# A hybrid decoder layer on one core: weight tiles as two half tiles, a planner constant for loads behind copies, and other buffers for the output projection's rows

## The chip, the cores and the metric

The kernel runs on one core of one Trainium2 chip. The metric is the device time of one execution in microseconds; the median of three runs counts.

## What is computed

One decoder layer on 1024 tokens of width 1024, in float32. The input is normalised, multiplied by one wide weight matrix, and its columns go to three branches and a gate:

```python
h = _rmsnorm(x, g_in[l])
proj = h @ w_in[l]
q_sb, k_sb, v_sb, u_c, b_c, c_c, q_mem, gate = jnp.split(proj, SPLIT_POINTS, axis=-1)
y_sb = _stick_breaking_attention(...)            # 8 heads of 64, strictly causal
y_conv = b_c * _causal_depthwise_conv(c_c * u_c, conv_w[l], conv_b[l])
m = _rmsnorm(mem, g_mem[l])
mk, mv = jnp.split(m @ w_mem_kv[l], 2, axis=-1)  # 256 memory tokens
y_mem = _memory_attention(...)                   # 4 heads of 64, softmax
y = jnp.concatenate([_rmsnorm(y_sb, g_sb_out[l]), _rmsnorm(y_conv, g_conv_out[l]),
                     _rmsnorm(y_mem, g_mem_out[l])], axis=-1)
x = x + (y * jax.nn.silu(gate)) @ w_out[l]
return _rmsnorm(x, g_final)
```

The weight of a stick-breaking head is A[t,s] = sigmoid(z_ts) times the product of 1 - sigmoid(z_tj) over the keys j between s and t.

## The kernel before

**The order is made by a planner.** The functions of the kernel don't issue instructions: each call is recorded as an `Op` with an engine (or two to choose from, `nc.either`: VectorE or GpSimd), a priority `prio`, and the ops that it needs. `Plan.lay_out` then plays the program through once with modelled durations: whenever an engine is idle it takes, of the ops whose inputs are there and whose tiles have a free buffer (`room`), the one with the lowest `prio`. `emit` issues the instructions in that order, so each engine has a fixed order when the kernel runs, and a wait of one instruction holds back all that stand behind it on its engine. Buffers of one tag are given out in the order of the program (`turn`, `nth`), except for tiles marked `loose`.

**The model of a DMA.** All DMAs are issued by SyncE. One of them takes `ISSUE` on SyncE, then its bytes go over one modelled wire, behind those before it, at the first of `RATES` (405, in KB per us) from or to DRAM and at the second (225) between two places of SBUF; `LANDING` comes on top.

**The work.** Matmuls are made more exact by splitting each operand in a high and a low part (`hi` is a rounded copy made by ScalarE, `lo` the rest, made by VectorE or GpSimd) and adding three products. A projection (`proj`) is one weight tile of 128 columns: `load_w` loads 512 KB into `wraw` (one buffer), splits it by halves into `whi` and `wlo` (two buffers each), and 48 matmuls of 512 columns add into two PSUM banks `pj`. At the start (the loop over `KC`) x comes in eight chunks; the first q and k projections (`w0`) and half of the values grow chunk by chunk.

Attention goes by pairs of heads. For a head, `stacks` copies q and k from natural layout (`qh`, `ql`, `kh`, `kl`) into the tiles `q`, `qs` and `k` by DMAs within SBUF, 256 KB each. `scores` makes score matmuls into PSUM banks `z` (two), sigmoids on ScalarE, a scan on VectorE; `apply` transposes the result through banks `tr` and multiplies with the values into banks `av` (two). Projections stand as fill between them, at a later priority (`FILL`).

`stats` sums the squares of one row block of y with a matmul by ones into a PSUM bank (`z`, loose); ScalarE reads it and four small DMAs spread the sums. `gate` is a projection whose evacuation multiplies with y. The last gate runs over the chunks of x one after another, so that the buffers `X` of x come free as it goes.

The end is the output projection. Each of eight row blocks of `w_out` is loaded into a raw buffer named by `RAW` (tags qh, ql, qh, ql, whi, whi, wlo, wlo), split into `woh` and `wol`, which from the second block on lie in buffers `X`, and 8 token blocks `j` are multiplied with all of them into the banks pj, z and tr.

Of the kernel before, what the change touches and what calls it, by code (L numbers as in the profile page):

```python
# [24 lines left out]
F32 = mybir.dt.float32  # L25
# [132 lines left out]
class Op:  # L158
    __slots__ = ("n", "engines", "call", "args", "kw", "prio", "needs", "then", "left", "tiles", "ready",
                 "table", "start", "engine", "nbytes", "cost", "port", "at")  # L160

# [19 lines left out]

ISSUE, RATES, LANDING, UNDER_WAY = 0.6, (405.0, 225.0), 1.35, 8
PATIENCE = 2.5


class Plan:
# [7 lines left out]
    def record(self, engines, call, args, kw):  # L194
# [41 lines left out]
        if call == "matmul":  # L236
            width = int(np.prod(kw["rhs"].shape[1:]))
            o.cost = {"tensor": width * 0.00042 + 0.014 if width > P else 0.1}
        elif call == "transpose":
            o.cost = {"tensor": 0.089}  # L240
        elif call == "dma_start":
            o.cost = {engines[0]: ISSUE}
            inside = all(isinstance(kw[x], View) and kw[x].tile.pool.name != "dram" for x in ("in_", "out"))
            o.nbytes = o.nbytes / 1024 / RATES[inside]
        elif call == "memset":
            o.cost = {e: 0.1 + 0.0011 * width for e in engines}
        else:
            pointers = sum(isinstance(kw.get(k), View) for k in ("scale", "bias"))
            wide = max([width] + [int(np.prod(v.shape[1:])) for v in ins]) if call == "tensor_reduce" else width
            o.cost = {"vector": 0.16 + 0.00105 * wide, "gpsimd": 0.18 + 0.00218 * wide,  # L250
                      "scalar": 0.18 + 0.00086 * wide + (0.09 if pointers else 0) + (0.2 if "accum_out" in kw else 0)}
            if call == "tensor_tensor_scan":
                o.cost = {"vector": 0.16 + 0.00208 * width}
            elif call == "scalar_tensor_tensor":
                o.cost = {e: c + 0.06 for e, c in o.cost.items()}
            elif kw.get("op") == ALU.pow:
                o.cost["gpsimd"] = 0.8 + 0.12 * width

            o.port = engines[0] in ("vector", "gpsimd") and len(ins) > 1 and not inpsum
# [4 lines left out]
    def lay_out(self):  # L264
# [3 lines left out]
        idle = dict.fromkeys(ready, 0.0)  # L268
        events, table, wire, landed = [], None, 0.0, []
        done, now, port = 0, 0.0, {"vector": 0.0, "gpsimd": 0.0}  # L270
# [38 lines left out]
        while done < len(self.ops):  # L309
            for e in ready:  # L310
                while idle[e] <= now:
# [22 lines left out]
                    if o.call == "dma_start":  # L334
                        wire = max(wire, begin + ISSUE) + o.nbytes
                        end = wire + LANDING
                        landed.append(end)
                    else:
                        end = begin + cost
# [44 lines left out]
def hymba_kernel(ctx, tc, xT, xr, wp, wv, memT, memr, wmem, cols, eye, wout, gfin, out):  # L384
# [3 lines left out]
    xpool = Pool(nc, "xpool", {"X": 16})  # L388
    wring = Pool(nc, "wring", {"wraw": 1, "whi": 2, "wlo": 2})
    stg = Pool(nc, "stg", {"stg": 4})  # L390
# [64 lines left out]
    w0 = []  # L455
    for pool, tag in ((wring, "wraw"), (att, "k")):
        w0.append((pool.tile([P, KC, P], F32, tag, "w0"), wring.tile([P, KC, P], F32R, "whi"),
                   wring.tile([P, KC, P], F32R, "wlo")))
    ps0 = [[bank("z"), bank("z")], [bank("pj"), bank("pj")]]
    for k in range(KC):  # L460
# [11 lines left out]
        for n in range(2):  # L472
            if k in (0, 2, 4):
                c = slice(k, KC if k == 4 else k + 2)
                nc.sync.dma_start(out=w0[n][0][:, c], in_=wp[4 * n][:, c])
        for n, c in enumerate(parts):
# [7 lines left out]
        if k in (0, 2, 4):  # L484
            for raw, hi, lo in w0:
                c = slice(k, KC if k == 4 else k + 2)
                nc.scalar.copy(hi[:, c], raw[:, c])
# [8 lines left out]
        def column(n, i):  # L496
            for a, (ww, xx) in enumerate(((w0[n][1], h), (w0[n][1], l), (w0[n][2], h))):
                nc.tensor.matmul(ps0[n][i], lhsT=ww[:, k, :], rhs=xx[:, HALVES[i]], start=(k == 0 and a == 0),
                                 stop=(k == KC - 1 and a == 2))
# [39 lines left out]
    fills = [0]  # L539

    def load_w(src, shape, prio=None, raw=None):
        prio = prio or SPLIT + fills[0]
        hi = wring.tile(shape, F32R, "whi")
        lo = wring.tile(shape, F32R, "wlo")
        raw = att.tile(shape, F32, raw, "wraw") if raw else wring.tile(shape, F32, "wraw")
        n = shape[1] // 2
        parts = [slice(0, n), slice(n, 2 * n)]
        for c, x in zip(parts if isinstance(src, list) else [slice(0, 2 * n)], src if isinstance(src, list) else [src]):
            nc.sync.dma_start(out=raw[:, c], in_=x, prio=prio)
        for c in parts:  # L550
            nc.scalar.copy(hi[:, c], raw[:, c], prio=prio)
            nc.either.tensor_tensor(lo[:, c], raw[:, c], f(hi[:, c]), op=ALU.subtract, prio=prio)
        return hi, lo

    def more_values():
# [3 lines left out]
        for jj in range(4):  # L559
            ps = bank("pj")  # L560
            for j in (2 * jj, 2 * jj + 1):
                for k in range(KC):
                    wh, wl = w[k // 4]
                    for a, (xx, ww) in enumerate(((xh, wh), (xh, wl), (xl, wh))):
                        nc.tensor.matmul(ps[:, (j % 2) * 256 : (j % 2 + 1) * 256], lhsT=xx[k][:, j * P : (j + 1) * P],
                                         rhs=ww[:, k % 4, :], start=(k == 0 and a == 0), stop=(k == KC - 1 and a == 2),
                                         prio=FILL + fills[0] + 0.1 * jj)
# [5 lines left out]
    def proj(n, evac, after=(), both=False):  # L573
# [7 lines left out]
        for i, k in steps:  # L581
            hf = HALVES[i]
            for a, (ww, xx) in enumerate(((wh, xh), (wh, xl), (wl, xh))):
                first = k == 0 and a == 0
                nc.tensor.matmul(ps[i], lhsT=ww[:, k, :], rhs=xx[k][:, hf], start=first,
                                 stop=(k == KC - 1 and a == 2), prio=FILL + fills[0] + (0 if both else 0.4 * i),
# [146 lines left out]
    def stats(c, late=False):  # L733
# [5 lines left out]
        for n, hf in enumerate(HALVES):  # L739
# [5 lines left out]
            nc.either.tensor_tensor(lo, s, f(hi), op=ALU.subtract)  # L745
            ps = psum.tile([P, H], F32, "z", loose=True)
            for b, w in enumerate((hi, lo)):
# [88 lines left out]
    def mem_kv():  # L836
# [10 lines left out]
        for k2 in range(4):  # L847
# [13 lines left out]
            for m in range(2):  # L861
                for kk in range(2):
                    for a, (ww, mm) in enumerate(((wh, mh), (wl, mh), (wh, ml))):
                        nc.tensor.matmul(acc[m], lhsT=mm[:, kk, m * P : (m + 1) * P], rhs=ww[:, kk, :],
                                         start=(k2 == 0 and kk == 0 and a == 0), stop=(k2 == 3 and kk == 1 and a == 2))
# [83 lines left out]
    woh, wol = [None] * 8, [None] * 8  # L949
    RAW = [(att, t) for t in ("qh", "ql", "qh", "ql")] + [(wring, t) for t in ("whi", "whi", "wlo", "wlo")]  # L950
    for n, c in enumerate(order):
# [3 lines left out]
        lo = pool.tile([P, D], F32R, tag, "wol")  # L955
        raw = RAW[n][0].tile([P, D], F32, RAW[n][1], "wor")
        nc.sync.dma_start(out=raw, in_=wout[c])
        for hf in HALVES:
            nc.scalar.copy(hi[:, hf], raw[:, hf])
            nc.either.tensor_tensor(lo[:, hf], raw[:, hf], f(hi[:, hf]), op=ALU.subtract)  # L960
        woh[c], wol[c] = hi, lo
# [97 lines left out]
```

## Time and profile before

| what | value |
|---|---|
| runs, us | 566.96, 568.11, 568.99 |
| median, us | 568.11 |
| profiled execution, us | 569.42 |
| its span, from the first to the last instruction, us | 567.4 |
| mean granted TensorE clock of the span | 0.996 |
| TensorE matmuls, share of the span | 97% |
| VectorE, ScalarE, GpSimd, share of the span | 73%, 63%, 33% |
| DMA queue of SyncE, share of 16 engines' span | 35.8% |

The profile shows one execution. Matmuls are pipelined: each is shown from its start to a modelled end, and neighbours overlap, so that the distance of two starts tells what a matmul takes. All instructions that the planner issues carry one line number, so groups are told apart by the tiles that they write and read (written <- read).

### The profile page before, as it was taken

What the parts mean: (1) busy time and instruction counts of PE and PEld (TensorE: products, weight loads), DVE (VectorE), ACT (ScalarE), POOL (GpSimd) and SP (SyncE); (2) the same over time, 40 slices, a digit from 0 to 9 for tenths busy, and PEclk for the clock granted to TensorE, in tenths of its full rate; (3) what the DMA queues carried; (4) which work ended last, traced back from release to release, by engine and by line L of the source; (5) the groups of instructions that cost most, each with busy time, mean ns of one, the idle gap of its engine ahead of it and who ended that gap; (6) DMA issues with size and microseconds to landing.
All of it is one profiled execution on the core that took longest, in us unless ns stands there. A gap on an engine that the chain in (4) does not pass through costs nothing.

```text
span 567.4 us, 8661 instructions
## 1 busy us (share of the span) xinstructions
PE 552.4 (97%) x2984; PEld 467.4 (82%) x2984; DVE 415.6 (73%) x658; ACT 355.9 (63%) x726; POOL 186.5 (33%) x214
## 2 busy tenths in 40 slices
PE   8999899999999999999899999999999999999995
PEld 6998789998888888888788878888878686888884
DVE  3345488878888798767497778769787678876673
ACT  5834577787677674785378797765689945332322
POOL 1220133332445534532063363212533239010010
PEclk9999999999999999999999999999999999999998
DMA  8953915043160711017732511443511342223301
GB/s 264 396 162 80 218 38 131 20 92 97 37 149 1 185 39 37 13 42 161 189 99 75 131 38 53 96 109 95 170 39 37 88 141 107 74 75 112 112 37 74
DMA packets 30655, 58.35 MB, mean 103 GB/s; under 512 B 13202, under 2 KB 14226, under 8 KB 30612
## 3 DMA queue, kind: packets, MB, share of 16 engines
q1 hardware_dynamic: 30612, 57.81, 35.8%
q8 instruction: 23, 0.38, 0.3%
q14 instruction: 20, 0.16, 0.1%
HBM read 36.78 MB, written 4.20 MB: 72 GB/s over the span
## 4 chain that ended last, share of the span: by engine, by line
PE 84%; DMA 6%; issue 3%; DVE 2%; ACT 2%; SPq 2%; POOL 1%; POOLq 0%; DVEq 0%; ACTq 0%
PE pj L380 49%; PE tr L380 14%; PE z L380 12%; PE av L380 9%; SPq L380 2%; DMA xs<-in_xT 2%; DMA q<-ql 1%; DMA stg<-in_wv 1%; DMA wraw<-in_wmem 1%; DMA gf<-in_gfin 1%; DVE stg L380 1%; DVE wlo L380 0%; ACT whi L380 0%; POOL wlo L380 0%; DMA part<-sq 0%
## 5 line engine op out<-in xcount | busy, mean ns | idle before, releaser
L380 PE MATMUL pj<-xh,whi 128*128 128x512 f32 x368 | 146.0, 397 | 1.2 <-DVE y L380 1.2
L380 PE MATMUL pj<-xl,whi 128*128 128x512 f32 x368 | 146.3, 398 | 0.0
L380 PE MATMUL pj<-xh,wlo 128*128 128x512 f32 x368 | 145.2, 395 | 0.0
L380 POOL TENSOR_TENSOR sg<-sg,F 128x512 f32<-128x512 f32 (+5 forms) x58 | 63.2, 1095 | 87.8 <-DVE F L380 60.1
L380 PEld LDWEIGHTS pj<-xh,whi 128*128 128x128 f32 x368 | 69.2, 188 | 14.5 <-DVE y L380 1.7
L380 PEld LDWEIGHTS pj<-xh,wlo 128*128 128x128 f32 x368 | 69.3, 188 | 12.3 <-issue 0.2
L380 PEld LDWEIGHTS pj<-xl,whi 128*128 128x128 f32 x368 | 69.3, 188 | 11.9 <-issue 0.2
L380 ACT ACTIVATE sg<-z,rq 128x511 f32<-128x511 f32 (+2 forms) x96 | 56.0, 583 | 36.1 <-PE z L380 31.3
L380 DVE TENSOR_TENSOR_SCAN F<-z,mask 128x512 f32<-128x512 f32 (+2 forms) x64 | 60.5, 949 | 19.4 <-ACT z L380 15.3
L380 POOL TENSOR_TENSOR wlo<-wraw,whi 128x512 fp32r<-128x512 f32 x32 | 43.9, 1380 | 79.8 <-ACT whi L380 76.8
L380 DVE TENSOR_TENSOR wtl<-tr,wth 128x512 fp32r<-128x512 f32 (+1 forms) x96 | 59.0, 638 | 10.6 <-ACT wth L380 10.1
L380 ACT CAST wth<-tr 128x512 fp32r<-128x512 f32 (+1 forms) x96 | 49.5, 551 | 18.2 <-PE tr L380 17.8
L380 ACT ACTIVATE z<-z,nrq 128x512 f32<-128x512 f32 (+3 forms) x96 | 53.3, 555 | 2.4
L380 PE MATMUL tr<-ident,sg 128*128 128x128 f32 x288 | 47.4, 273 | 0.0
L380 PE MATMUL av<-wth,vh 128*128 128x256 f32 (+1 forms) x160 | 42.8, 277 | 0.0
L380 PE MATMUL av<-wtl,vh 128*128 128x256 f32 (+1 forms) x160 | 41.3, 292 | 0.5 <-DVE wtl L380 0.5
L380 PEld LDWEIGHTS tr<-ident,sg 128*128 128x128 f32 x288 | 34.5, 140 | 3.4 <-POOL sg L380 0.2
L380 PE MATMUL z<-k,q 128*128 128x512 f32 (+2 forms) x96 | 34.3, 359 | 3.2 <-issue 1.7
L380 ACT CAST whi<-wraw 128x512 fp32r<-128x512 f32 x56 | 32.3, 619 | 7.8 <-DMA wraw<-in_wp 4.5
L380 DVE TENSOR_TENSOR_SCAN F<-z,F,mask 128x511 f32<-128x511 f32 (+1 forms) x32 | 32.3, 1010 | 3.4 <-ACT z L380 2.1
L380 ACT ACTIVATE junk<-acc 128x512 f32<-128x512 f32 (+1 forms) x17 | 10.3, 607 | 38.9 <-DVE acc L380 38.1
L380 DVE TENSOR_TENSOR wlo<-wraw,whi 128x512 fp32r<-128x512 f32 x24 | 28.1, 1174 | 7.2 <-ACT whi L380 7.2
(171 smaller groups left out, 1199.3 us busy)
## 6 DMA issues: line engine op xcount, KB each, us to landing
wraw<-in_wp SPq DMA_DIRECT2D x22, 512.0 KB, 3.4
rows<-in_xr SPq DMA_DIRECT2D x8, 512.0 KB, 8.2
wor<-in_wout SPq DMA_DIRECT2D x8, 512.0 KB, 3.4
acc<-in_xr SPq DMA_DIRECT2D x8, 512.0 KB, 3.3
out<-acc SPq DMA_DIRECT2D x16, 256.0 KB, 2.3
xs<-in_xT SPq DMA_DIRECT2D x6, 512.0 KB, 8.8
q<-qh SPq DMA_DIRECT2D x12, 256.0 KB, 2.9
q<-ql SPq DMA_DIRECT2D x12, 256.0 KB, 4.1
```

What stands on the lines that cost most here:

```text
L380: f(*[real(x) for x in o.args], **{k: real(x) for k, x in o.kw.items()})
```

## The change

- `SWITCH = 2.2`: the planner lets a DMA that is not a large copy within SBUF (over 64 KB) wait 2.2 us more on the modelled wire when the DMA before it was such a copy.
- The tags `wraw`, `whi`, `wlo` get twice as many buffers of half the size. A weight tile is a pair of tiles of 4 chunks (class `Halves`), each loaded by a DMA of its own (256 KB), split as before, and freed by itself. `w0` at the start is cut in the same way; its raw tiles lie in `F` and `wraw` instead of `wraw` and `k`.
- The bank of `stats` is taken from `av` instead of `z`.
- The raw rows of `w_out` lie in qh, ql, kl, wraw, whi, qh, wlo, ql; those in wraw, whi and wlo are loaded by halves.

```diff
+SWITCH = 2.2
...
-            o.nbytes = o.nbytes / 1024 / RATES[inside]
+            o.nbytes, o.inside = o.nbytes / 1024 / RATES[inside], inside and o.nbytes > 65536
...
-        events, table, wire, landed = [], None, 0.0, []
+        events, table, wire, landed, was = [], None, 0.0, [], False
...
-                        wire = max(wire, begin + ISSUE) + o.nbytes
+                        wire = max(wire, begin + ISSUE) + o.nbytes + (SWITCH if was and not o.inside else 0.0)
+                        was = o.inside
...
-    wring = Pool(nc, "wring", {"wraw": 1, "whi": 2, "wlo": 2})
+    wring = Pool(nc, "wring", {"wraw": 2, "whi": 4, "wlo": 4})
...
-    for pool, tag in ((wring, "wraw"), (att, "k")):
-        w0.append((pool.tile([P, KC, P], F32, tag, "w0"), wring.tile([P, KC, P], F32R, "whi"),
-                   wring.tile([P, KC, P], F32R, "wlo")))
+    for n in range(2):
+        w0.append([[pool.tile([P, KC // 2, P], dt, tag, "w0") for _ in range(2)]
+                   for pool, dt, tag in ((wring if n else att, F32, "wraw" if n else "F"),
+                                         (wring, F32R, "whi"), (wring, F32R, "wlo"))])
...
+    class Halves:
...
+        def __init__(self, make, shape):
+            self.n = shape[1] // 2
+            self.parts = [make([P, self.n, *shape[2:]]) for _ in range(2)]
+
+        def __getitem__(self, k):
+            return self.parts[k // self.n][:, k % self.n]
...
     def load_w(src, shape, prio=None, raw=None):
         prio = prio or SPLIT + fills[0]
-        hi = wring.tile(shape, F32R, "whi")
-        lo = wring.tile(shape, F32R, "wlo")
-        raw = att.tile(shape, F32, raw, "wraw") if raw else wring.tile(shape, F32, "wraw")
-        n = shape[1] // 2
-        parts = [slice(0, n), slice(n, 2 * n)]
-        for c, x in zip(parts if isinstance(src, list) else [slice(0, 2 * n)], src if isinstance(src, list) else [src]):
-            nc.sync.dma_start(out=raw[:, c], in_=x, prio=prio)
-        for c in parts:
-            nc.scalar.copy(hi[:, c], raw[:, c], prio=prio)
-            nc.either.tensor_tensor(lo[:, c], raw[:, c], f(hi[:, c]), op=ALU.subtract, prio=prio)
+        hi, lo = (Halves(lambda sh: wring.tile(sh, F32R, t), shape) for t in ("whi", "wlo"))
+        if raw:
+            raw = att.tile(shape, F32, raw, "wraw")
+            rows = [raw[:, slice(n * hi.n, (n + 1) * hi.n)] for n in range(2)]
+        else:
+            rows = Halves(lambda sh: wring.tile(sh, F32, "wraw"), shape).parts
+        for n in range(2):
+            x = src[n] if isinstance(src, list) else src[:, slice(n * hi.n, (n + 1) * hi.n)]
+            nc.sync.dma_start(out=rows[n], in_=x, prio=prio)
+            nc.scalar.copy(hi.parts[n], rows[n], prio=prio)
+            nc.either.tensor_tensor(lo.parts[n], rows[n], f(hi.parts[n]), op=ALU.subtract, prio=prio)
         return hi, lo
...
-            ps = psum.tile([P, H], F32, "z", loose=True)
+            ps = psum.tile([P, H], F32, "av", loose=True)
...
-    RAW = [(att, t) for t in ("qh", "ql", "qh", "ql")] + [(wring, t) for t in ("whi", "whi", "wlo", "wlo")]
...
-        raw = RAW[n][0].tile([P, D], F32, RAW[n][1], "wor")
-        nc.sync.dma_start(out=raw, in_=wout[c])
-        for hf in HALVES:
-            nc.scalar.copy(hi[:, hf], raw[:, hf])
-            nc.either.tensor_tensor(lo[:, hf], raw[:, hf], f(hi[:, hf]), op=ALU.subtract)
+        home = ("qh", "ql", "kl", "wraw", "whi", "qh", "wlo", "ql")[n]
+        if home[0] != "w":
+            raw = att.tile([P, D], F32, home, "wor")
+            nc.sync.dma_start(out=raw, in_=wout[c])
+            raw = [raw[:, hf] for hf in HALVES]
+        else:
+            raw = [wring.tile([P, H], F32, home, "wor") for _ in HALVES]
+            for r, hf in zip(raw, HALVES):
+                nc.sync.dma_start(out=r, in_=wout[c][:, hf])
+        for r, hf in zip(raw, HALVES):
+            nc.scalar.copy(hi[:, hf], r)
+            nc.either.tensor_tensor(lo[:, hf], r, f(hi[:, hf]), op=ALU.subtract)
```

The matmuls take their weights from the halves (`ww[k // 4][:, k % 4]` at the start, `ww[k]` later) and are otherwise the same.

## Rows read from the trace of the kernel before

**Rows 1.** The page's busy times: engine, busy us (share of the span), instructions.
```profile
PE 552.4 (97%) x2984; PEld 467.4 (82%) x2984; DVE 415.6 (73%) x658; ACT 355.9 (63%) x726; POOL 186.5 (33%) x214
```
**Rows 2.** TensorE by time, 278 to 281.5: start, us, operation, shape, count [idle before].
```profile
278.09 0.39 PE L380 MATMUL pj<-xh,wlo 128*128 128x512 f32 x1
280.16 0.47 PE L380 MATMUL z<-k,q 128*128 128x512 f32 x1 [1.68 <-issue]
...
281.16 0.39 PE L380 MATMUL pj<-xh,whi 128*128 128x512 f32 x1
281.39 0.40 PE L380 MATMUL pj<-xl,whi 128*128 128x512 f32 x1
```
**Rows 3.** What TensorE waited for: us in total, times, longest us.
```profile
PE pj L380 <- DVE y L380: 2.0, 2, 1.2
PE z L380 <- issue: 1.7, 1, 1.7
PE z L380 <- DMA q<-ql: 1.5, 1, 1.5
...
PE av L380 <- DVE wtl L380: 0.5, 1, 0.5
```
**Rows 4.** TensorE by time, 472 to 475.1, the start of the output projection.
```profile
472.29 0.39 PE L380 MATMUL z<-woh,yl 128*128 128x512 f32 x1
473.27 1.02 PE L380 MATMUL tr<-woh,yh 128*128 128x512 f32 x2 [0.59 <-ACT woh L380]
475.05 0.50 PE L380 MATMUL pj<-woh,yh 128*128 128x512 f32 x1 [0.76 <-DVE y L380]
```
**Rows 5.** TensorE by time, 60.4 to 63.
```profile
60.47 0.39 PE L380 MATMUL pj<-xl,whi 128*128 128x512 f32 x1
62.33 0.70 PE L380 MATMUL z<-k,q 128*128 128x512 f32 x2 [1.48 <-DMA q<-ql]
62.87 0.40 PE L380 MATMUL pj<-xh,wlo 128*128 128x512 f32 x1
```
**Rows 6.** VectorE by time, at 270.5.
```profile
270.52 1.27 DVE L380 TENSOR_TENSOR wlo<-wraw,whi 128x512 fp32r<-128x512 f32 x1
```
**Rows 7.** SyncE's DMA issues by time, 270 to 275: the time is that of issuing.
```profile
270.90 1.10 SPq L380 DMA_DIRECT2D k<-kh  x2
272.11 0.55 SPq L380 DMA_DIRECT2D wraw<-in_wp  x1
272.75 1.63 SPq L380 DMA_DIRECT2D k<-kl  x2
```
**Rows 8.** DMA issues from 270.8 to 276: size, median us from issue to landing.
```profile
k<-kh SPq DMA_DIRECT2D x2, 256.0 KB, 3.9
wraw<-in_wp SPq DMA_DIRECT2D x1, 512.0 KB, 6.7
```
**Rows 9.** SyncE's DMA issues by time, 35 to 53.
```profile
35.38 0.33 SPq L380 DMA_DIRECT2D wraw<-in_wp  x1
...
52.27 0.50 SPq L380 DMA_DIRECT2D wraw<-in_wp  x1
```
**Rows 10.** ScalarE by time, at 49.3.
```profile
49.29 1.14 ACT L380 CAST whi<-wraw 128x512 fp32r<-128x512 f32 x2
```
**Rows 11.** DMA issues from 287.2 to 289.5, as rows 8.
```profile
wraw<-in_wp SPq DMA_DIRECT2D x1, 512.0 KB, 3.4
stg<-in_memr SPq DMA_DIRECT2D x2, 256.0 KB, 2.7
```
**Rows 12.** ScalarE by time, at 469.9.
```profile
469.94 1.14 ACT L380 CAST woh<-wor 128x512 fp32r<-128x512 f32 x2 [3.65 <-DMA wor<-in_wout]
```
**Rows 13.** TensorE and ScalarE by time, 137 to 138.5: one sum of squares.
```profile
137.10 0.63 PE L380 MATMUL z<-sq,ones 128*2 128x512 f32 x2
...
137.77 0.57 ACT L380 COPY sq<-z 1x512 f32<-1x512 f32 x1 [1.78 <-PE z L380]
```
**Rows 14.** VectorE by time, at 444.9.
```profile
444.91 0.69 DVE L380 TENSOR_SCALAR gf<-gf 128x1024 f32<-128x1024 f32 x1 [1.93 <-DMA gf<-in_gfin]
```

More of the change, by code (lines that the diff above doesn't have):

```diff
@@ L159 @@
     __slots__ = ("n", "engines", "call", "args", "kw", "prio", "needs", "then", "left", "tiles", "ready",
-                 "table", "start", "engine", "nbytes", "cost", "port", "at")
+                 "table", "start", "engine", "nbytes", "cost", "port", "at", "inside")
 def views(args, kw):
@@ L474, in hymba_kernel @@
                 c = slice(k, KC if k == 4 else k + 2)
-                nc.sync.dma_start(out=w0[n][0][:, c], in_=wp[4 * n][:, c])
+                nc.sync.dma_start(out=w0[n][0][k // 4][:, c.start % 4 : c.start % 4 + c.stop - c.start], in_=wp[4 * n][:, c])
         for n, c in enumerate(parts):
@@ L484, in hymba_kernel @@
         if k in (0, 2, 4):
-            for raw, hi, lo in w0:
-                c = slice(k, KC if k == 4 else k + 2)
+            for raw, hi, lo in ((t[k // 4] for t in w) for w in w0):
+                c = slice(k % 4, 4 if k == 4 else k + 2)
                 nc.scalar.copy(hi[:, c], raw[:, c])
@@ L497, in column @@
             for a, (ww, xx) in enumerate(((w0[n][1], h), (w0[n][1], l), (w0[n][2], h))):
-                nc.tensor.matmul(ps0[n][i], lhsT=ww[:, k, :], rhs=xx[:, HALVES[i]], start=(k == 0 and a == 0),
+                nc.tensor.matmul(ps0[n][i], lhsT=ww[k // 4][:, k % 4], rhs=xx[:, HALVES[i]], start=(k == 0 and a == 0),
                                  stop=(k == KC - 1 and a == 2))
@@ L565, in more_values @@
                         nc.tensor.matmul(ps[:, (j % 2) * 256 : (j % 2 + 1) * 256], lhsT=xx[k][:, j * P : (j + 1) * P],
-                                         rhs=ww[:, k % 4, :], start=(k == 0 and a == 0), stop=(k == KC - 1 and a == 2),
+                                         rhs=ww[k % 4], start=(k == 0 and a == 0), stop=(k == KC - 1 and a == 2),
                                          prio=FILL + fills[0] + 0.1 * jj)
@@ L584, in proj @@
                 first = k == 0 and a == 0
-                nc.tensor.matmul(ps[i], lhsT=ww[:, k, :], rhs=xx[k][:, hf], start=first,
+                nc.tensor.matmul(ps[i], lhsT=ww[k], rhs=xx[k][:, hf], start=first,
                                  stop=(k == KC - 1 and a == 2), prio=FILL + fills[0] + (0 if both else 0.4 * i),
@@ L863, in mem_kv @@
                     for a, (ww, mm) in enumerate(((wh, mh), (wl, mh), (wh, ml))):
-                        nc.tensor.matmul(acc[m], lhsT=mm[:, kk, m * P : (m + 1) * P], rhs=ww[:, kk, :],
+                        nc.tensor.matmul(acc[m], lhsT=mm[:, kk, m * P : (m + 1) * P], rhs=ww[kk],
                                          start=(k2 == 0 and kk == 0 and a == 0), stop=(k2 == 3 and kk == 1 and a == 2))
```

## The prediction

> **What bounds the kernel.** I read the page's busy times first, then what TensorE waits for, then the order of time around each wait. TensorE is busy for 552.4 us, 97% of the span of 567.4 us [rows 1], and its matmuls follow one another: two neighbouring 512-column matmuls start 0.23 us apart though each is shown with 0.39 us, because they overlap [rows 2]. The diff adds, drops and reshapes no matmul. So the time can only move by the 15.0 us in which TensorE is idle, and by idle time of the same kind that a new order may add. The waits that the list names, beside the first matmul's, are 2.0 us for VectorE's y, 1.7 us "issue", 1.5 us for the copy q<-ql and 0.5 us for wtl [rows 3], and 0.6 us for woh [rows 4]: 6.3 us. The rest of the 15.0 us is the start and the end of the kernel, where the edits don't reach. The bounds are thus narrow downwards and open upwards.
>
> The two waits of score matmuls (z) have one look. In the first, TensorE starts a projection matmul at 278.09 and the next instruction, z<-k,q, only at 280.16: 2.07 - 0.23 = 1.84 us lost; then at 281.16 come projection matmuls of the next weight tile [rows 2]. In the second it goes from 60.47 to 62.33, 1.86 - 0.23 = 1.63 us lost, and projection matmuls follow at 62.87 [rows 5]. TensorE's order is fixed when the kernel is built, so it stands before z with other work behind it. That the work was ready I read from the split of the next tile: its last wlo began at 270.52 and took 1.27 us, so it was there at 271.8, 6 us before the wait [rows 6].
>
> Why z came late: SyncE put a 512 KB weight load between the copies k<-kh and k<-kl [rows 7]. The second k<-kh was issued at about 271.4 and landed 3.9 us later, at 275.3; the load, issued at 272.11, landed 6.7 us later, at 278.8 [rows 7, 8]. That is 3.5 us behind the copy. The planner counts 512 / 405 = 1.3 us for it (its constant RATES), so it is 2.2 us too early there, and the copies behind the load inherit that. The wait of 1.84 us fits: the plan put z about 2 us too early. The other one has the same load among its copies, at 52.27 [rows 9].
>
> **The change part by part, in the 569.42 us of the profiled execution** (span 567.4 us and 2.0 us around it; it is 0.2% above the median of the runs, 568.11).
>
> 1. The model's SWITCH of 2.2 us touches the plan alone: no instruction is new. The planner then sees the copies behind a load as late as they are and takes the projection matmuls first. Cover: at 278 a whole tile of 48 matmuls, 48 x 0.23 = 11 us, is ready; at 60.5 the rest of the tile that goes on at 62.87. I take both waits as gone: -1.84 - 1.63 = -3.47 us. Bounds: 0 (the planner takes the first ready instruction by priority, and another wait stands there) to -3.47.
>
> 2. Halves of weight tiles. The instructions of ScalarE, VectorE and GpSimd stay as they were (they split by halves already); a half of whi, wlo or wraw comes free without its other half. The first tile behind the start shows the worth: loaded at 35.38, split only from 49.29, because whi was held until the last chunk of the first two projections; the next load follows at 52.27, into the middle of the copies [rows 9, 10]. With halves in their own buffers, whi for chunks 0 to 3 is free when half of the chunks are done, the split moves ahead of 49.29 and the load ahead of the copies. This gives the copies room, but what they gain is the same 1.63 us again, so I add nothing. The price is 22 + 4 more loads and 3 more for rows of wout, 29 DMA issues on SyncE's queue, 0.33 to 0.55 us each [rows 7, 9]: 10 to 16 us of SyncE. Queued behind them are the stack copies, the sums' part rows and the next loads; SyncE's issues lie beside TensorE's work nearly everywhere, so I take 0. Where a copy that TensorE waits for is queued behind one more issue, it costs 0.55 us; there are two such places, the two z waits: bound 0 to +1.1.
> A row of 512 KB lands 3.4 us after its issue, one of 256 KB 2.7 us [rows 11]. If the second half overlaps the first, it lands about 2.7 + 0.4 = 3.1 us after the first issue; if not, 2 x 2.7 = 5.4 us. No wait of TensorE in the list is for a weight load, so either is hidden; the second is a rival below.
> The Trainium skill (SBUF — State Buffer, "The DMA setup-cost knee") speaks against halves: each transfer pays a fixed 2 us or so whatever its size, so transfers should be coalesced. The trace agrees on the fixed part (2 x 2.7 - 3.4 = 2.0 us). By that rule, with no overlap, 26 halved loads would add 26 x 2 = 52 us to the DMA queue, an estimate from that page; here they would count only where a weight is late.
>
> 3. Rows of wout. They wait for buffers. ScalarE sat 3.65 us until a row of wout landed and went on at 469.94 [rows 12]; the pool hands out woh tiles in program order, so the fourth row, whose raw buffer was the second's, held up the four behind it. In the change the fourth row goes to wraw, free once the last projection's raw weights are split, and the sixth to qh, free once the first row is split. TensorE's part: 472.29 to 475.05 holds three starts' worth of work, 2.76 - 0.69 = 2.07 us lost, in three pieces: 0.75 us before 473.27, 0.40 us inside the pair (1.02 us instead of 0.39 + 0.23), and 0.92 us before 475.05, which waits for y [rows 4]. The first two I take as gone, and of the third, which is the last gate's evacuation, half, since more rows ready means more matmuls to put there: -0.75 - 0.40 - 0.46 = -1.61 us. Bounds 0 to -2.07.
>
> 4. The sums' PSUM bank moves from z to av: same instructions. z gets two banks for scores alone; av is shared instead. The trace shows no such wait in either direction. Bound it by how long a sum holds its bank: from 137.10 to the end of ScalarE's read at 138.34, 1.24 us [rows 13], 16 times: -0.5 (the one av wait in the list) to +19.8. I take 0, the row nearest being that z is now read without a TensorE wait.
>
> 5. What a new order puts in. Every stage is planned anew, and waits like those for y and wtl fall elsewhere. One wait of 0.5 us [rows 3] for each of the three places that are replanned: +1.5 us. Bounds 0 to +5, the latter when all of the gain comes back.
>
> Sum: -3.47 - 1.61 + 1.5 = -3.6 us; 569.4 - 3.6 = 565.8 us for an execution like the profiled one, and 568.1 - 3.6 = 564.5 us as a median.
>
> **The rivals.**
> - All named waits go: -1.84 - 1.63 - 2.07 - 0.5 and the 1.2 us that is the larger of the two waits for y [rows 3]: -7.3 us, 560.8. For it: halves free buffers in every stage. Against: the 1.2 us comes from VectorE, which stood 1.93 us before scaling gf until its row landed [rows 14]; nothing in the change touches that.
> - The waits move: the greedy planner still puts some instruction on TensorE too early, as with gf, and only about 0.6 us is left: 567.5. For it: each wait in the list has another cause.
> - Slower, by the sums' bank. A sum takes one of two av banks for 1.24 us [rows 13] while attention sums hold the other; if the next av matmul stands first on TensorE then, all of the fill behind it stands too. Against: the planner counts free banks. It cancels gain and margin from (3.6 + 1.7) / 1.24 = 4.3 of 16 sums on; with 6, 7.4 - 3.6 = +3.8 us: 571.9.
> - Halves land one after the other: 5.4 - 3.4 = 2.0 us later each. With two projections late near the end, 4.0 - 3.6 = +0.4: 568.5.
> - The change does not do what it says: the planner's order is hardly touched; that is the second rival's time.
>
> **How the numbers follow.** 0.3%, 1.7 us, is about what a measurement of this kernel can tell from no change. The forecast has 0.43 (its own range 562.5 to 566.4), all waits gone 0.13, waits that move 0.22, late halves 0.05, the bank 0.17. Faster is 0.43 + 0.13 = 0.56, the same 0.22 + 0.05 = 0.27, slower 0.17. The range takes in the lower case with a little of the unnamed waits, 560.0, and the bank's case, 572.0; some 0.05 lie below and 0.1 above.
>
> **What would show it.** Right: no z wait over 0.5 us in the list of TensorE's waits; TensorE's idle time 3 to 4 us less than 15.0, with the same number of matmuls; the second weight load before the first copies at 51; no landing of a wout row behind the last gate's matmuls, and ScalarE without its 3.65 us. Wrong: a z wait beside a load that is still among the copies (step 1); a wait of TensorE for whi, wlo or wraw (step 2); av matmuls behind a read of a sum (step 4); or a longer wait for y (step 5).

## The result and the profile after

The changed kernel takes 561.77 us (median of 4 runs, 561.31 to 564.8) against 568.55 us of the kernel before: the ratio, taken over the single runs and not from the two medians, is 0.9897, 95% interval 0.9857 to 0.9937, or 3.6 to 8.1 us less. The profiled execution takes 561.93 us, its span is 560.1 us (before: 569.42 and 567.4). The forecast was faster, 564.5 us, in 560 to 572: the direction and the range held, the size was nearly twice the one forecast (6.8 us instead of 3.6).

The page's busy times of the changed kernel, to be set beside [rows 1], and its row of weight loads (number of DMAs, size, median us from issue to landing):

```profile
span 560.1 us, 8745 instructions
PE 550.0 (98%) x2984; PEld 468.7 (84%) x2984; DVE 405.8 (72%) x657; ACT 360.1 (64%) x728; POOL 181.5 (32%) x215
wraw<-in_wp SPq DMA_DIRECT2D x44, 256.0 KB, 3.0
```

The 2984 matmuls are the same. TensorE's idle time, span less busy time, went from 15.0 to 10.1 us: 4.9 of the 7.3 us by which the span is shorter. The other 2.4 us are in the busy time (552.4 to 550.0), although no matmul was dropped. Neighbouring matmuls overlap in the records [rows 2], so a start that is late by less than the overlap leaves no idle time: a delay hides in rows that count as busy. The measure without this gap is the distance from one matmul's start to the next, less the median distance of its shape, as the 2.07 - 0.23 of the prediction. Summed by stages of the span, worked out from the traces of both kernels (us lost):

```
stage        0-40  40-80  80-260  260-300  300-440  440-480   all
before       3.23   1.98    2.52     2.58     3.12     4.02  17.3
after        3.77   0.74    1.39     0.20     2.22     2.09  10.3
change      +0.54  -1.24   -1.13    -2.38    -0.90    -1.93  -7.0
```

(Behind 480 neither loses anything; the median distances alone add up to 542.0 us in both.) These 7.0 us are the 7.3 us of the span but for 0.3, which lies behind the last matmul's start. They are in five stages, while the prediction had put all of it into three: 40-80, 260-300 and 440-480.

What TensorE waited for in the changed kernel (us in total, times, longest), in answer to [rows 3]:

```profile
PE pj L383 <- DVE y L383: 1.4, 2, 0.8
PE tr L383 <- DVE onesf L383: 1.3, 1, 1.3
...
PE z L383 <- DMA q<-ql: 0.2, 1, 0.2
```

Of the two waits before scores, 1.7 and 1.5 us, 0.2 us is left. The entry for onesf is the first matmul's and is in both kernels. No wait for whi, wlo or wraw is in the list.

TensorE by time at the place of [rows 5] (start, us, operation, shape, count, idle before), and SyncE's issues that lead to it, in answer to [rows 9]:

```profile
58.97 0.39 PE L383 MATMUL pj<-xl,whi 128*128 128x512 f32 x1
59.56 0.70 PE L383 MATMUL z<-k,q 128*128 128x512 f32 x2 [0.20 <-DMA q<-ql]
```
```profile
42.55 0.88 SPq L383 DMA_DIRECT2D wraw<-in_wp  x2
51.03 1.15 SPq L383 DMA_DIRECT2D k<-kh  x2
52.23 0.62 SPq L383 DMA_DIRECT2D k<-kl  x1
52.90 0.96 SPq L383 DMA_DIRECT2D q<-qh  x1
53.90 0.82 SPq L383 DMA_DIRECT2D q<-ql  x1
```

The weight load that stood among the copies at 52.27 is now issued at 42.55, in two halves, 8.5 us ahead of the first copy, because ScalarE splits the first tile behind the start already at 40.52 and 41.31 instead of 49.29 [rows 10]:

```profile
40.52 0.62 ACT L383 CAST whi<-wraw 128x512 fp32r<-128x512 f32 x1 [1.80 <-DMA wraw<-in_wp]
41.31 0.62 ACT L383 CAST whi<-wraw 128x512 fp32r<-128x512 f32 x1 [0.17 <-DMA wraw<-in_wp]
```

Now the place of [rows 2 and 7], TensorE first, then SyncE:

```profile
279.45 0.39 PE L383 MATMUL pj<-xh,wlo 128*128 128x512 f32 x1
279.68 0.39 PE L383 MATMUL z<-k,q 128*128 128x512 f32 x1
279.90 0.39 PE L383 MATMUL z<-k,qs 128*128 128x512 f32 x1
```
```profile
268.99 0.46 SPq L383 DMA_DIRECT2D k<-kh  x1
269.57 0.51 SPq L383 DMA_DIRECT2D wraw<-in_wp  x1
270.18 0.88 SPq L383 DMA_DIRECT2D k<-kl  x1
```

A load still stands between k<-kh and k<-kl, as before, but z starts 0.23 us behind a projection matmul: here the load did not leave, TensorE was given other work until the copies had landed (the last k<-kl was issued at 272.07 and landed at 277.27). That load is now one of the halves, 256 KB. So the two waits went in two different ways, and the experiments ask which edit did which.

At the end of the last stage, TensorE in answer to [rows 4], and the casts of wout's rows on ScalarE (minimum, median and maximum ns, first and last start) in answer to [rows 12]:

```profile
467.63 0.39 PE L383 MATMUL tr<-woh,yh 128*128 128x512 f32 x1
467.86 0.39 PE L383 MATMUL tr<-wol,yh 128*128 128x512 f32 x1
468.08 0.39 PE L383 MATMUL tr<-woh,yl 128*128 128x512 f32 x1
468.31 0.39 PE L383 MATMUL tr<-woh,yh 128*128 128x512 f32 x1
469.37 0.50 PE L383 MATMUL pj<-woh,yh 128*128 128x512 f32 x1 [0.67 <-DVE y L383]
```
```profile
L383 ACT CAST woh<-wor x16: 603/616/626, 399.9 to 470.4; 128x512 fp32r<-128x512 f32 x16
```

The 0.75 and 0.40 us of late rows are gone, 1.06 - 0.23 = 0.83 us for the last gate's y are left. ScalarE has no wait for a row of wout in this stage.

### The profile page after: what moved, and what is told of

It is laid out like the page before. It is cut to its first block, busy times and chain, and to the rows that moved or that the text cites. A ratio compares the mean times of both kernels' runs of the same rounds, so it can differ in the third digit from the quotient of the medians.

```text
span 560.1 us, 8745 instructions
## 1 busy us (share of the span) xinstructions
PE 550.0 (98%) x2984; PEld 468.7 (84%) x2984; DVE 405.8 (72%) x657; ACT 360.1 (64%) x728; POOL 181.5 (32%) x215
## 4 chain that ended last, share of the span: by engine, by line
PE 88%; DMA 4%; ACT 2%; issue 2%; DVE 2%; SPq 1%; POOLq 0%; POOL 0%; ACTq 0%
PE pj L383 52%; PE tr L383 14%; PE z L383 12%; PE av L383 10%; DMA xs<-in_xT 2%; DMA stg<-in_wv 1%; DMA q<-ql 1%; SPq L383 1%; DVE stg L383 0%; ACT L383 0%; ACT vh L383 0%; DVE y L383 0%; ACT pj L383 0%; ACT z L383 0%; DVE xl L383 0%
## 5 line engine op out<-in xcount | busy, mean ns | idle before, releaser
L383 PE MATMUL pj<-xh,whi 128*128 128x512 f32 x352 | 139.4, 396 | 0.8 <-DVE y L383 0.8
L383 PE MATMUL pj<-xh,wlo 128*128 128x512 f32 x352 | 139.8, 397 | 0.0
L383 PE MATMUL pj<-xl,whi 128*128 128x512 f32 x352 | 139.4, 396 | 0.0
L383 PEld LDWEIGHTS pj<-xh,whi 128*128 128x128 f32 x352 | 66.2, 188 | 13.3 <-DVE y L383 1.3
L383 PEld LDWEIGHTS pj<-xh,wlo 128*128 128x128 f32 x352 | 66.2, 188 | 12.3 <-issue 0.3
L383 PEld LDWEIGHTS pj<-xl,whi 128*128 128x128 f32 x352 | 66.2, 188 | 12.0 <-issue 0.2
L383 POOL TENSOR_TENSOR wlo<-wraw,whi 128x512 fp32r<-128x512 f32 x36 | 48.5, 1349 | 82.3 <-ACT whi L383 75.6
L383 PE MATMUL tr<-ident,sg 128*128 128x128 f32 x288 | 48.9, 273 | 0.0
L383 ACT CAST whi<-wraw 128x512 fp32r<-128x512 f32 x56 | 34.1, 621 | 15.1 <-PE pj L383 11.1
L383 PEld LDWEIGHTS av<-wth,vh 128*128 128x128 f32 x160 | 30.3, 189 | 3.3
```

The costliest lines, as they stand in the source:

```text
L383: f(*[real(x) for x in o.args], **{k: real(x) for k, x in o.kw.items()})
```

## The experiments

Theory: the planner's SWITCH removes both score waits, the new row list removes the wait at the end, halves and the bank change nothing of their own. Rivals: the halves remove the waits by moving loads; or the whole difference is the luck of a new order, since a changed plan can move waits that have nothing to do with the edit. The kernel before was measured beside the others on the same chip; its medians were 568.96 us for experiments 1 to 4, 569.43 for 5 to 8 and 569.12 for 9 to 12.

**1. SWITCH alone.** The hunks of SWITCH put into the kernel before:

```diff
+SWITCH = 2.2
-            o.nbytes = o.nbytes / 1024 / RATES[inside]
+            o.nbytes, o.inside = o.nbytes / 1024 / RATES[inside], inside and o.nbytes > 65536
-                        wire = max(wire, begin + ISSUE) + o.nbytes
+                        wire = max(wire, begin + ISSUE) + o.nbytes + (SWITCH if was and not o.inside else 0.0)
+                        was = o.inside
```

> The kernel before with the planner's SWITCH alone; whole weight tiles, sums in z, rows of w_out where they were. Theory of the model's mistake: both z waits (1.84 us at about 278, 1.63 us at about 60) go, the rest stays within 1 us, so 568.5 - 3.5 = 565.0 us. Rival, halves are what counts: the load still stands among the copies, z is only moved and waits elsewhere, so 567 to 569 us. Rival, any new plan draws new waits: 565 to 572 us, with waits at places that have nothing to do with copies.

Measured: 574.27 us, 1.0082 [1.0052, 1.0113]: slower. The load stays among the copies (52.61), the planner takes the projection matmuls first, as it should, and z does not wait. But the next projection then stands at a result of the last one that VectorE has not taken out of PSUM yet. SyncE, TensorE and VectorE, by time:

```profile
51.29 1.15 SPq L382 DMA_DIRECT2D k<-kh  x2
52.61 0.47 SPq L382 DMA_DIRECT2D wraw<-in_wp  x1
53.19 0.92 SPq L382 DMA_DIRECT2D k<-kl  x1
```
```profile
63.08 0.62 PE L382 MATMUL z<-k,q 128*128 128x512 f32 x2
...
64.21 0.39 PE L382 MATMUL pj<-xh,wlo 128*128 128x512 f32 x1
64.44 0.61 PE L382 MATMUL z<-k,qs 128*128 128x512 f32 x2
66.15 0.47 PE L382 MATMUL pj<-xh,whi 128*128 128x512 f32 x1 [1.10 <-DVE kl L382]
```
```profile
64.64 0.70 DVE L382 TENSOR_TENSOR pj<-pj,rb 128x512 f32<-128x512 f32 x1 [2.71 <-PE pj L382]
65.31 1.37 DVE L382 TENSOR_TENSOR kl<-pj,kh 128x512 fp32r<-128x512 f32 x2
```

The matmuls that filled the wait for the copies at 60 are those that would have filled the evacuation at 64.6: 13 of the tile were left behind z before, 4 are left here. The wait has moved from the copy to VectorE's kl. In the kernel before the same kl itself stood for a copy, one of those behind the load, and was done at 66.18:

```profile
65.49 0.69 DVE L380 TENSOR_TENSOR kl<-pj,kh 128x512 fp32r<-128x512 f32 x1 [3.00 <-DMA k<-kl]
```

The next tile began at 66.31 there, without a wait, and begins at 66.15 here: with the load still among the copies, the other order of TensorE gained next to nothing at this place. The stage loses 2.36 us (before 1.98). 260-300 loses 1.17 instead of 2.58, but experiment 4 will show 1.48 with the order of before, so this is no proof of SWITCH. 80-260 loses 6.59 instead of 2.52: 2.4 us in one wait for wtl, which ends at 145.86, and 1.5 us right behind it, at 147.0 to 150.4, where the granted clock of TensorE was 0.50, its lower level (1.2 GHz).

**2. Halves alone.** The changed kernel with three edits taken back:

```diff
-SWITCH = 2.2
+SWITCH = 0.0
-            ps = psum.tile([P, H], F32, "av", loose=True)
+            ps = psum.tile([P, H], F32, "z", loose=True)
-        home = ("qh", "ql", "kl", "wraw", "whi", "qh", "wlo", "ql")[n]
+        home = ("qh", "ql", "qh", "ql", "whi", "whi", "wlo", "wlo")[n]
```

> The changed kernel with SWITCH 0, sums back in z and the rows of w_out by the old list: half tiles alone. Theory of the model's mistake: the load at 52 us moves ahead of the copies, so the z wait at 60 goes (1.6 us), but the one at 278 stays at 1.5 to 2 us: 568.5 - 1.6 = 566.9 us. Rival, halves are what counts: both z waits and the small waits go, 563 us or less. Rival, any new plan: 565 to 572 us.

Measured: 570.72 us, 1.0032 [1.0006, 1.0058]. Its stage 40-80 is that of the changed kernel (0.73), and the load is ahead of the copies, by SyncE's issues:

```profile
42.44 0.88 SPq L383 DMA_DIRECT2D wraw<-in_wp  x2
51.30 1.15 SPq L383 DMA_DIRECT2D k<-kh  x2
```

260-300 loses 2.51 us, as before. What made it slower is the end, 6.71 us in 440-480: TensorE stands for a row of wout whose load lands late; TensorE, then ScalarE:

```profile
471.36 0.39 PE L383 MATMUL z<-woh,yl 128*128 128x512 f32 x1
473.99 0.50 PE L383 MATMUL tr<-woh,yh 128*128 128x512 f32 x1 [2.24 <-ACT woh L383]
```
```profile
471.23 0.62 ACT L383 CAST woh<-wor 128x512 fp32r<-128x512 f32 x1 [5.42 <-DMA wor<-in_wout]
```

Behind this stand, from 474.8 to 478.2, the granted clock was 0.50 (the number before the last two in the first row, a row of busy times by engine), and matmuls of 512 columns started 0.43 us apart instead of 0.23:

```profile
474.80:478.20 3.40, 3.05 (x7) 2.47 (x8) 3.40 (x4) 3.28 (x8) 3.40 (x3) 0.50 0.02 5
```
```profile
475.74 0.63 PE L383 MATMUL pj<-wol,yh 128*128 128x512 f32 x1
476.17 0.63 PE L383 MATMUL pj<-woh,yl 128*128 128x512 f32 x1
```

That is 1.5 of the 6.71 us. So the halves remove the wait at 60 without SWITCH, and a gain of 1.3 us there is lost again at the end.

**3. The bank alone.** In the kernel before: `-"z", loose=True` / `+"av", loose=True` for the sums' tile.

> The kernel before with the bank of the sums in av instead of z, nothing else. Forecast of step 4: no change, 568 to 569 us, both z waits still there. Rival, the sums hold an av bank: TensorE waits for av, 6 times 1.24 us, 576 us. Rival, any new plan: other waits, 565 to 572 us.

Measured: 568.33 us, 0.9982 [0.9952, 1.0012]: no difference that can be told. ScalarE's wait for a row of wout is still there (3.70 us, at 470.16), yet the end stage loses 2.15 us instead of 4.02, and 300-440 loses 5.13 instead of 3.12. Most of the difference at the end is not at the rows: the 1.4 us that TensorE lost at 445 for VectorE's y are gone, as VectorE, which stood for the row of gf before [rows 14], scales it at 439.64 there, ahead of that evacuation; at the rows 1.30 us are lost instead of 2.07. The expectation that both z waits stay was half wrong: 260-300 loses 0.50 us, without SWITCH and without halves.

**4. The row list alone.** In the kernel before, with whole tiles:

```diff
-    RAW = [(att, t) for t in ("qh", "ql", "qh", "ql")] + [(wring, t) for t in ("whi", "whi", "wlo", "wlo")]
+    RAW = [(wring if t[0] == "w" else att, t) for t in ("qh", "ql", "kl", "wraw", "whi", "qh", "wlo", "ql")]
```

> The kernel before with the raw rows of w_out in qh, ql, kl, wraw, whi, qh, wlo, ql, as whole rows. Step 3: ScalarE's wait of 3.65 us for a row at 469.9 goes, TensorE's lost 2.07 us at 472 to 475 become 0.5 to 1.0: 568.5 - 1.3 = 567.2 us; everything ahead of about 395 us is the same as before. Rival, the last gate's evacuation sets that wait: it stays at 2 us, 568.5 us.

Measured: 566.79 us, 0.9960 [0.9935, 0.9985]: 2.3 us less. ScalarE's casts of wout run in one piece, and TensorE loses 0.70 - 0.23 = 0.47 us at the end instead of the 2.07 of [rows 4]:

```profile
463.21 5.31 ACT L380 CAST woh<-wor 128x512 fp32r<-128x512 f32 x10 [1.02 <-PE pj L380]
```
```profile
474.57 0.39 PE L380 MATMUL tr<-woh,yh 128*128 128x512 f32 x1
475.27 0.50 PE L380 MATMUL pj<-woh,yh 128*128 128x512 f32 x1 [0.31 <-DVE y L380]
```

The rows are planned late, and TensorE's order in this kernel is that of the kernel before up to 470.7. So it is a second execution of that order, and the wait at 278 is another one in it, 0.54 - 0.23 = 0.31 us instead of 1.84:

```profile
278.82 0.39 PE L380 MATMUL pj<-xh,wlo 128*128 128x512 f32 x1
279.36 0.47 PE L380 MATMUL z<-k,q 128*128 128x512 f32 x1 [0.15 <-issue]
```

The load among the copies landed 2.4 us behind the second k<-kh here (278.24 and 275.83), against 3.5 us in the profile from which the prediction took the 2.2 us of SWITCH. At 52 the distance is steady: 3.65 to 3.85 us in before and in experiments 1, 3 and 4.

The four edits alone give +0.82, +0.32, -0.18 and -0.40%, a sum of +0.56%; together they give -1.03%. They do not add, and the gain is in what they do to one another. The next four take one edit away from the whole.

**5. All but the bank.** The changed kernel with the sums back in z (the second hunk of experiment 2).

> The changed kernel with the sums back in z. Step 4: no price and no gain, so as the changed kernel within 2 us, 560 to 564 us. Theory of luck (each plan draws its own waits, about 14 to 22 us of lost starts in the kernels so far): anything from 562 to 572 us, with new waits at places without a sum. Theory that z and av matter: TensorE waits on z beside the sums, 564 to 567 us.

Measured: 562.89 us, 0.9886 [0.9867, 0.9905]: as the whole.

**6. All but SWITCH.** The changed kernel with SWITCH at 0.0.

> The changed kernel with SWITCH 0. Theory of the model's mistake: a z wait of about 1 to 2 us comes back at 270 to 280, so 561.8 + 1.5 = 563.3 us. Theory of luck: 562 to 572 us, and the waits that are new stand beside no load. SWITCH alone made the kernel before slower by 0.8%; if it is harmful in itself, this one is faster than 561.8.

Measured: 563.97 us, 0.9909 [0.9890, 0.9928]. The interval overlaps those of the whole (0.9897) and of experiment 5, so a price of SWITCH cannot be told from the time. (Experiment 12 and experiment 5 differ by SWITCH alone too: 0.9930 and 0.9886, with intervals that overlap by little.) The trace shows it: 260-300 loses 2.07 us instead of 0.20. The largest waits there are no longer z's (0.17 us for k<-kl) but those of transposes for VectorE's sg, 0.9 us in two.

**7. All but the row list.** The changed kernel with the old list (the third hunk of experiment 2).

> The changed kernel with the rows of w_out in qh, ql, qh, ql, whi, whi, wlo, wlo (the last four by halves). Everything up to about 390 us as in the changed kernel. Step 3: rows come late behind the last gate, TensorE loses 2 to 4.5 us more at 460 to 476, so 564 to 566 us, as it did with halves alone (4.9 us lost there). If the rows don't matter: 562 us.

Measured: 562.64 us, 0.9887 [0.9869, 0.9904]: as the whole; 440-480 loses 2.74 us against 2.09.

**8. All but the halves.** The kernel before with the edits of experiments 1, 3 and 4.

> The kernel before with SWITCH, the sums in av and the new rows as whole tiles: all but the halves. If halves and SWITCH need each other (SWITCH makes the planner bring z later; only halves have the fill ready): as SWITCH alone less the rows, 572 us. If the parts add up: 568.6 + 4.7 - 1.0 - 2.2 = 570.1 us. Theory of luck: 563 to 574 us.

Measured: 567.76 us, 0.9964 [0.9938, 0.9990]. That is no more than the row list's gain alone (0.9960). As in experiment 1, TensorE's list of waits has the projection that stands for VectorE's kl, and wtl:

```profile
PE pj L382 <- DVE kl L382: 1.3, 1, 1.3
PE av L382 <- DVE wtl L382: 1.3, 1, 1.3
```

So the halves, which the prediction gave no gain, are the edit without which most of it isn't there: 0.9964 against 0.9897.

**9 to 11. How much is luck?** A constant of the planner that has nothing to do with the edits, a margin in its event times, set a little higher in the kernel before, the whole change, and the halves alone:

```diff
-SLACK = 0.3
+SLACK = 0.33
```

> The kernel before with one constant of the planner that has no part in the change moved by a tenth (SLACK 0.33 instead of 0.30 us): a new plan with the same buffers, rows and DMA model. Theory of luck: the time moves as far as the parts of the change moved it, 1 to 6 us either way, 563 to 574 us. Theory that the parts themselves set the time: within 1.5 us of before, 567 to 570 us, with the two z waits still there, because the model still knows nothing of the load among the copies.

> The changed kernel with SLACK 0.33. Theory of luck: 561.8 was a good draw, so this is worse, 563 to 570 us. Theory that half tiles with the rest set the level: 561 to 564 us, as the three kernels that leave one other part out.

> Half tiles alone, with SLACK 0.33. Half tiles alone were slower than before (570.7 us). If that was a bad draw of the plan: 563 to 566 us here. If half tiles alone are really no gain: 568 to 572 us.

Measured: before 570.64 us, 1.0024 [0.9996, 1.0053]; the whole 564.01, 0.9895 [0.9860, 0.9931]; halves alone 570.19, 1.0001 [0.9977, 1.0026]. A new order by itself moved these three by up to 0.3%. The level of the whole change stays, 0.9895 beside 0.9897, so it is not luck. Single waits are: with the halves alone, the wait at 278 comes back larger than it was. Of the two half loads there, one was issued at 272.35, 1.15 us ahead of k<-kh, the other at 274.73, behind the k<-kl (274.14) that z waits for, so none stands between the two copies; TensorE by time:

```profile
274.78 0.39 PE L383 MATMUL pj<-xh,wlo 128*128 128x512 f32 x1
278.08 0.47 PE L383 MATMUL z<-k,q 128*128 128x512 f32 x1 [2.91 <-DMA k<-kl]
```

**12. Halves with the row list,** without SWITCH and with the sums in z (the first two hunks of experiment 2).

> Half tiles and the new rows, without SWITCH and with the sums in z. Half tiles alone lost 4.9 us at 460 to 476, against 2.2 us in the kernel before. If the old rows were the cause: that becomes 1 us, 570.7 - 4 = 566.7 us. If any two of the parts beside the halves are needed: 568 to 570 us. Theory of luck: anything from 563 to 572 us.

Measured: 566.00 us, 0.9930 [0.9900, 0.9959]. Against the halves alone (570.72 and 570.19) the end stage went from 6.71 and 5.35 (1.5 and 1.7 of them at the lower clock) to 2.43 us lost; 260-300 stays at 2.82, as SWITCH isn't there.

All kernels, us lost by TensorE's starts, in the stages that tell them apart, worked out as above:

```
                     halves SWITCH bank rows   40-80  80-260  260-300  300-440  440-480
before                 -      -     z   old     1.98    2.52     2.58     3.12     4.02
before, SLACK          -      -     z   old     4.06    2.04     1.59     4.77     4.71
SWITCH alone           -      x     z   old     2.36    6.59     1.17     3.82     4.83
bank alone             -      -     av  old     2.04    3.14     0.50     5.13     2.15
rows alone             -      -     z   new     1.52    2.54     1.48     3.42     2.02
all but halves         -      x     av  new     2.37    3.60     0.52     4.43     1.09
halves alone           x      -     z   old     0.73    1.68     2.51     3.52     6.71
halves alone, SLACK    x      -     z   old     0.68    1.56     3.38     3.59     5.35
halves and rows        x      -     z   new     0.65    1.68     2.82     3.48     2.43
all but SWITCH         x      -     av  new     0.67    1.49     2.07     5.43     0.99
all but rows           x      x     av  old     0.69    1.41     0.20     2.18     2.74
all but bank           x      x     z   new     0.68    2.31     0.21     4.42     0.33
after                  x      x     av  new     0.74    1.39     0.20     2.22     2.09
after, SLACK           x      x     av  new     0.72    1.44     0.17     4.79     1.32
```

Two things must be known before it is read. Each row is one execution, and kernels that differ in a late edit share TensorE's order up to it: before and rows alone up to 470, halves alone and halves and rows up to 469, after and all but rows up to 459. Where the order is the same, the figures differ by up to 1.1 us (2.58 and 1.48 at 260-300), so a smaller difference between two rows alone tells nothing. And in five of the executions the granted clock was 0.50 for a stretch inside the span, each time behind a stand of TensorE, which puts 1.5 to 1.7 us into one entry: 40-80 of before with SLACK (4.06, at 63.9 to 67.3), 80-260 of SWITCH alone (6.59), 440-480 of both kernels with halves alone (6.71 and 5.35), and 0-40 of all but halves, which is not shown.

Read down the columns. 40-80: 0.65 to 0.74 in all eight kernels with halves, 1.52 to 4.06 in the six without (to 2.6 but for the clock), whatever SWITCH is. 260-300: 0.17 to 0.21 in the four kernels with halves and SWITCH, 2.07 to 3.38 in the four with halves and no SWITCH; without halves it lies anywhere between 0.50 and 2.58. 440-480: 4.02 to 6.71 (3.7 to 5.2 but for the clock) in the five kernels with old rows and the sums in z, at most 2.74 in the nine others. 80-260: a median of 1.5 with halves and 2.8 without, with one overlap (2.31 and 2.04). 300-440: no edit sorts it, 2.2 to 5.4 us.

## Why the prediction was right, and where it was not

**What bounds the kernel.** It held: the same matmuls, and the span moved by their late starts alone. That only 15.0 us of idle time were to be had was too narrow: 17.3 us were lost, 2.4 us of what was gained lay inside busy rows, and 7.9 of the 15.0 us stand ahead of the first matmul and behind the last.

**Step 1, SWITCH, -3.47 us.** The amount came (both waits went: of 1.63 us, 0.59 - 0.23 = 0.36 is left, of 1.84 nothing), the cause was half wrong. This is the step that failed. The prediction named as cover at 60 "the rest of the tile" and did not ask what that rest had covered until then. In SWITCH alone TensorE takes it at once and stands 1.10 us at 66.15 for VectorE's kl, at the place where the next tile began before (66.31). The lower end of the bounds, 0 for "another wait stands there", was the truth for SWITCH by itself, and even this end was too good: it reached 0.8% above before. At 278 the reasoning did hold, once the halves are there: 0.2 us lost with SWITCH, 2.07 or more without (of which 0.33 to 3.07 ahead of z, and in three of the four 1.2 ahead of transposes). But 1.84 us was a high price for that wait: the same order lost 0.31 us there in another execution, and with the bank alone, whose order is another, it is not there either.

**Step 2, halves, 0 us.** The mechanism was described as it came: whi free earlier, the split ahead of 49.29, the load ahead of the copies. The conclusion that it is "the same 1.63 us again" credited SWITCH with it, and the runs give it to the halves. On top they take about 1.1 us out of 80-260, for which the prediction had no term. The price was rightly zero: 22 more loads of projection weights (44 for 22) and no wait for a weight (all but the bank has two for wlo, 0.5 us together); all 29 added issues took 14.2 us more of SyncE, inside the 10 to 16 of the prediction. The two halves of the load at 42.55 land 2.62 and 2.91 us after issues 0.54 us apart, thus 0.54 + 2.91 = 3.45 us after the first issue; a whole tile took 3.4 [rows 11]. The rival with halves one behind the other, 5.4 us, fell. The Trainium skill (SBUF — State Buffer, "The DMA setup-cost knee") states a fixed 2 us or so for every transfer. The 52 us that the prediction worked out from it, on the condition of no overlap, did not come: these two transfers were under way together, and the second half landed when a whole tile would have (3.45 and 3.4 us).

**Step 3, the rows of wout, -1.61 us.** By itself it held: 2.3 us by the ratio, 2.00 in the stage 440-480, 1.60 of them in the very pieces named (2.07 to 0.47). In the whole it is worth nothing that can be measured (0.9887 without it). The bank alone also takes that stage down, from 4.02 to 2.15, 0.77 of it at the rows; with neither edit, the halves make it worse (6.71, of which TensorE's stand for the row is 2.4 and the lower clock behind it 1.5). The prediction had not looked at the edits together. Of the third piece half was taken as gone, 0.46 us; of 0.92, 0.83 is left. (By starts the third piece was 1.02 us and the second 0.30, as the second tr of the pair began at 473.80; the sum is the same.)

**Step 4, the bank, 0 us, bounds -0.5 to +19.8.** Held: no price with it alone (0.9982), none in the whole (0.9897 with, 0.9886 without), no wait of an av matmul in the list after. The slower rival fell with it. That it shortens the end stage was not seen. In the bank alone ScalarE's late row is still there (3.70 us) and TensorE loses less by it; the larger part, 1.4 us, is VectorE's earlier scaling of gf, and whether that comes of the bank or of one new order is not shown.

**Step 5, new waits, +1.5 us.** Wrong in sign for the whole: 80-260 and 300-440 lose 2.03 us less. In 300-440 it is luck, since the same change with another SLACK loses 4.79 instead of 2.22 and takes 0.9895 all the same. In SWITCH alone the allowance would have been right, and too small (80-260: +4.1 us, of which 1.5 at the lower clock).

**The rivals.** By the size, "all named waits go" (560.8) was nearer than the forecast. The objection to it was that nothing in the change touches the row of gf [rows 14]. That was wrong: VectorE scales gf at 440.43 now without waiting. Yet TensorE still stands for y there, because VectorE waits for ScalarE's pj; VectorE, then TensorE, in the changed kernel:

```profile
440.43 0.68 DVE L383 TENSOR_SCALAR gf<-gf 128x1024 f32<-128x1024 f32 x1
...
445.05 0.69 DVE L383 TENSOR_TENSOR stg<-stg,y 128x512 f32<-128x512 f32 x1 [1.17 <-ACT pj L383]
```
```profile
446.59 0.50 PE L383 MATMUL pj<-xh,whi 128*128 128x512 f32 x1 [0.78 <-DVE y L383]
```

"The waits move" (567.5) is what happens without the halves: 567.76 was measured for all but them. So the direction came out partly by luck: what the prediction credited to SWITCH at 60 came because the halves were in the same change. The size was too small, as 1.5 us were added for waits that did not come and nothing was forecast for 80-260 and 300-440.

What stays open: why VectorE scales gf earlier with the other bank, which waits make up the 1.1 us that halves take out of 80-260, and how far the medians of the kernels differ by the clock behind a stand, which the profiles show for one execution each.

## What to carry to other kernels

Before an in-order engine is given other work to fill a wait, ask what that work was filling until now: at 60 it was the cover of the next evacuation, and the wait only changed its name, while at 278 a whole tile was spare and it worked. Buffers that come free in smaller pieces can do what a better model cannot, as they let a transfer leave the place where it collides; but their worth may show only with the edits beside them, so take one away from the whole as well as adding one alone. Where a planner lays everything anew, run each kernel with an indifferent constant moved, and believe the level, and the stages that repeat, rather than a single wait: the 1.84 us with which SWITCH was credited at 278 were 0.31 in another execution of the same order.

## What the runs showed of the hardware

Two 256 KB loads issued 0.54 us apart land within 3.45 us of the first issue, the time of one 512 KB load (3.4 us); another pair, 0.39 us apart at 35.97, took 5.25 us where the whole tile of the kernel before took 5.0; in the whole kernel 44 halves land 3.0 us after issue in the median and delay no matmul. Copies within SBUF that queue up land later and later: in the changed kernel q<-ql, the fifth 256 KB copy of a row, lands 5.5 us after its issue, and those behind it about 1.1 us apart (62.71, 63.78, 64.84). A 512 KB load from DRAM issued behind a copy within SBUF landed 2.4 to 3.85 us after that copy, in the kernel before and in experiments 1, 3 and 4. A stand of TensorE can cost more than its length: in five executions the granted clock was 0.50 (1.2 GHz) for a stretch that began 0.7 to 1.2 us behind the end of a stand, and 512-column matmuls started 0.43 us apart there, 1.5 to 1.7 us in all; the stands were 2.2 to 2.6 us, in one case 1.7 and 1.0 us close together. It is no rule: behind the 2.91 us at 278 with halves alone and SLACK 0.33 the clock stayed at 1.00 until 474.7. And TensorE's busy share hides late starts: of the 7.3 us by which the span is shorter 2.4 were in rows that counted as busy, since each 512-column matmul is shown with 0.39 us and its successor starts after 0.23.
